# Turning one of the five long expert turns of a mixture-of-experts layer into a short one

## The chip, the cores and the metric

The kernel runs on one core of a Trainium2 chip, as one program. The metric is the device time of one execution in microseconds, as the median of several runs. Five engines matter here: TensorE (PE, with its weight loads PEld), VectorE (DVE), ScalarE (ACT), GpSimd (POOL) and SyncE (SP), whose queue issues nearly all transfers from HBM. "Weight load" is used below only for PE's own loads; what SP brings from HBM is called a load of expert weights.

## The reference, cut to what matters

A two-layer network on 256 tokens of width 1024 (and 256 context tokens in layer 0). Layer 1 ends with eight experts, of which each token takes two. Everything is in float32.

```python
def swiglu(h, w1, w3, w2):
    return (jax.nn.silu(h @ w1) * (h @ w3)) @ w2

def moe_swiglu(h, router_w, w1, w3, w2):
    t = h.reshape(B * L, D)                       # 256 x 1024
    logits = (t @ router_w).astype(jnp.float32)
    top_v, top_i = lax.top_k(logits, TOP_K)       # TOP_K = 2
    gates = jax.nn.softmax(top_v, axis=-1)
    ...
    for e in range(N_EXPERTS):                    # w1, w3: 1024 x 3584, w2: 3584 x 1024
        out = out + combine[:, e:e + 1] * swiglu(t, w1[e], w3[e], w2[e])
```

256 tokens with two experts each make 512 pairs, 64 an expert on average.

## The kernel before, in words

The program first computes layer 0 and the mixer of layer 1, and then the eight experts in eight **turns**, 0 to 7, one expert a turn. Before the first turn has gone far, a plan made on the chip (`plan`) counts the tokens of each expert and hands the experts to the turns. Expert 0 always has turn 0, since its weights are on the way before the router is done; the others are ranked by their number of tokens, and `RANKS` says which rank goes to which turn.

A turn has room for 128 or 64 tokens, by the table `TURNS`. The code of the two kinds differs:

- In a **long** turn (128) float32 products are made of three products of split numbers. The raw weights of a load are copied by ACT to a rounded high part (`hi`) and subtracted by DVE to a low part (`lo`); PE multiplies the tokens' high part by `hi` and by `lo` (lines 1590 and 1591) and the tokens' low part by `hi` (line 1594). The down products are the three lines of `mm3` (156 to 158). Raw room is free for the next load when DVE has made `lo`.
- In a **short** turn (64) there is no split: PE multiplies the raw float32 weights, with the 64 tokens in one half of the array's columns for one half of a load and in the other half for the other (lines 1582 and 1614). Raw room is free when PE has multiplied.

An expert's weights come in four chunks of its 3584 hidden columns (1024, 1024, 1024, 512). The turn goes over the chunks: the up products of chunk c with `w1` and `w3`, then the down products of the chunk before it with `w2`; the down products of a turn's last chunk come after the next turn's first up products. Each load is 1 MB, 42 loads a turn whatever its kind. `gather` collects the next turn's tokens during chunk 2, `finish` spreads a turn's rows back to the tokens (`macc`) during the first chunks of the next turn.

SP issues the loads strictly in the order of use. Their room is a ring of 12 tiles of 1 MB (`rr` and `raw`; 14 at first and 11 late in the last turn), so that a load is issued when the load 12 places ahead of it has let go of its room. In a long turn the high parts are made for up to two loads beyond the one that PE works on (`AHI`), the low parts for one (`ALO`).

```python
NRM, NHM, NLM, AHI, ALO = 12, 3, 2, 2, 1
            while len(his) + len(ahead) < AHI:
            while his and len(ahead) < ALO:
```

After the eight turns the program looks at two numbers of the plan: by how many tokens the fullest turn exceeds its room, and whether an expert has more than 128. If the first is above 0, a **second pass** computes all eight experts anew, with room for 128 in every turn (`tc.If(over > room)`).

Of the kernel before, what the change touches and what calls it, by code (L numbers as in the profile page):

```python
# [31 lines left out]
NHB = 4  # L32


TURNS = (128, 64, 128, 128, 64, 128, 128, 64)
LONG, SHORT = iter((0, 1, 2, 3, 4)), iter((5, 6, 7))
RANKS = [next(LONG) if n == 128 else next(SHORT) for n in TURNS]

CHUNKS = [(0, 1024), (1024, 1024), (2048, 1024), (3072, 512)]
# [3 lines left out]
def host_consts():  # L43
# [16 lines left out]
    i8 = np.arange(8)  # L60
    rt = np.concatenate([(i8[None, :] < i8[:, None]).reshape(-1), np.arange(1, 129), RANKS, TURNS, i8, 1024 * (i8 == 0)])
    return {
# [9 lines left out]
def hybrid_kernel(ctx: ExitStack, tc: tile.TileContext, a: dict, out: bass.AP, dbg=None, upto="end"):  # L72
# [1677 lines left out]
    def by_number(t, e):  # L1750
        return pm[:, t, e:e + 1]

    expert_pass(0, TURNS, number, by_turn,
                lambda t, e: comb[:, t, 0:1] if e == 0 else turns[:, 2 + t, e:e + 1])
# [39 lines left out]
```

## Time and profile before

| what | value |
|---|---|
| median of 3 runs | 1711.8 us (1709.98 to 1712.49) |
| the profiled execution | 1708.4 us |
| its span (first to last instruction) | 1706.6 us |
| granted TensorE clock, mean over the span | 0.992 of full speed |
| PE busy | 1653.8 us (97%) |
| DVE busy | 1152.3 us (68%) |
| ACT busy | 810.9 us (48%) |
| HBM read | 476.37 MB, 280 GB/s over the span |

Busy PE is not PE at its peak, because the records of overlapping matmuls are laid end to end, and the shares are means over a long front part (to about 796 us) and the eight expert turns after it. The table therefore says little about the turns; for these the rows below go stretch by stretch.

### The profile page before, as it was taken

The page shows a single profiled execution, that of the slowest core. Times are in us where ns is not written, and L with a number is a line of the kernel's source. Part 1 is how long each engine was busy: PE and PEld are TensorE (multiplying, and loading weights), DVE is VectorE, ACT ScalarE, POOL GpSimd, SP SyncE. Part 2 cuts the span into 40 slices and gives each one's busy share as a digit, 9 for nine tenths or more (in the row PEclk, how much of TensorE's full clock was granted, in tenths as well). Part 3 has the DMA queues.
Part 4 walks back from the last instruction along what each step waited for, and adds up shares of the span by engine and source line. Part 5 has one row for each costly group of instructions (what it writes and reads, how often), then busy time and mean ns, then how long its engine had stood idle before and what let it go on. Part 6 is the DMA issues. An engine that isn't in the chain of part 4 may idle for free.

```text
span 1706.6 us, 22066 instructions
## 1 busy us (share of the span) xinstructions
PE 1653.8 (97%) x8284; PEld 1238.7 (73%) x8284; DVE 1152.3 (68%) x1372; ACT 810.9 (48%) x941; POOL 26.8 (2%) x51
## 2 busy tenths in 40 slices
PE   7989999999999999999999999999999999999995
PEld 3767888788888888877786367888853578888532
DVE  3698897788566666856984148889841488898322
ACT  4633455322221357455773046777730467777201
POOL 1000000000000000000000000000000000000000
PEclk9999999999999999999999999999999999999997
DMA  9433375555565445337999999999999999999995
GB/s 367 150 101 123 99 253 162 167 187 174 184 198 185 152 145 179 113 132 283 327 357 337 409 410 412 408 411 376 342 354 408 412 411 409 411 375 347 355 406 197
DMA packets 186797, 479.03 MB, mean 281 GB/s; under 512 B 11761, under 2 KB 65201, under 8 KB 172081
## 3 DMA queue, kind: packets, MB, share of 16 engines
q1 hardware_dynamic: 185040, 473.80, 75.7%
q10 hardware_dynamic: 1074, 2.72, 0.5%
q8 instruction: 69, 1.13, 0.3%
q0 software_dynamic: 560, 0.94, 0.2%
q14 instruction: 54, 0.44, 0.1%
HBM read 476.37 MB, written 1.05 MB: 280 GB/s over the span
## 4 chain that ended last, share of the span: by engine, by line
PE 87%; DVE 5%; DMA 4%; ACT 2%; issue 1%; SPq 1%; POOL 0%; DVEq 0%; ACTq 0%; POOLq 0%
PE mm L156 9%; PE mm L157 8%; PE mm L158 8%; PE h L1582 8%; PE h L1591 7%; PE h L1594 7%; PE h L1590 7%; PE y L156 6%; PE y L157 6%; PE y L158 6%; PE y L1614 2%; DMA raw<-moe_w 2%; PE sc L589 1%; DMA rr<-moe_w 1%; PE sc L1561 1%
## 5 line engine op out<-in xcount | busy, mean ns | idle before, releaser
L145 ACT ACTIVATE hi<-raw 128x1024 fp32r<-128x1024 f32 x127 | 134.5, 1060 | 310.2 <-PE mm L157 99.0
L177 DVE TENSOR_TENSOR rb<-raw,rb 128x2048 fp32r<-128x2048 f32 x86 | 196.5, 2289 | 57.3 <-ACT rb L177 39.2
L1591 PE MATMUL h<-rb,hg 128*128 128x512 f32 x560 | 218.8, 391 | 2.6 <-DVE rb L177 2.5
L149 DVE TENSOR_TENSOR lo<-raw,hi 128x1024 fp32r<-128x1024 f32 x127 | 155.3, 1224 | 88.6 <-ACT hi L145 85.4
L177 ACT ACTIVATE rb<-raw 128x2048 fp32r<-128x2048 f32 x86 | 165.0, 1918 | 63.5 <-PE h L1594 28.5
L422 DVE SCALAR_TENSOR_TENSOR rr<-rr,cs,rr 128x512 f32<-128x512 f32 x256 | 181.8, 747 | 10.1 <-DMA rr<-b_mod 4.6
L156 PE MATMUL mm<-hbk,hi 128*128 128x512 f32 (+1 forms) x456 | 166.5, 366 | 0.9 <-DVE tm L829 0.8
L157 PE MATMUL mm<-hbk,hi 128*128 128x512 f32 (+1 forms) x456 | 163.7, 359 | 0.5 <-DVE hbk L305 0.5
L158 PE MATMUL mm<-hbk,lo 128*128 128x512 f32 (+1 forms) x456 | 163.7, 359 | 0.0
L177 DVE TENSOR_TENSOR rb<-rr,rb 128x2048 fp32r<-128x2048 f32 x50 | 114.4, 2290 | 34.0 <-ACT rb L177 24.1
L1590 PE MATMUL h<-rb,hg 128*128 128x512 f32 x352 | 130.9, 393 | 0.0
L1591 PEld LDWEIGHTS h<-rb,hg 128*128 128x128 f32 x560 | 105.1, 188 | 27.9 <-DVE rb L177 4.6
L177 DVE TENSOR_TENSOR rb<-raw,part 128x2048 fp32r<-128x2048 f32 x51 | 116.7, 2288 | 10.0 <-ACT part L177 4.3
L177 DVE TENSOR_TENSOR sil<-sil,h 128x512 f32<-128x512 f32 (+1 forms) x47 | 31.4, 669 | 127.2 <-PE h L1582 112.5
L177 ACT ACTIVATE part<-raw 128x2048 fp32r<-128x2048 f32 x51 | 97.7, 1916 | 39.7 <-PE h L1594 16.6
L177 ACT ACTIVATE rb<-rr 128x2048 fp32r<-128x2048 f32 x50 | 95.9, 1918 | 37.5 <-PE h L1594 15.7
L157 PE MATMUL y<-rb,ht 128*128 128x512 f32 x280 | 109.7, 392 | 0.0
L1594 PE MATMUL h<-rb,hg 128*128 128x512 f32 x352 | 107.0, 390 | 2.5 <-DVE hg L177 2.5
L1582 PE MATMUL h<-raw,hgs 128*64 128x512 f32 (+1 forms) x512 | 103.9, 541 | 0.0
L156 PEld LDWEIGHTS mm<-hbk,hi 128*128 128x128 f32 x456 | 85.8, 189 | 16.2 <-issue 2.4
L157 PEld LDWEIGHTS mm<-hbk,hi 128*128 128x128 f32 x456 | 86.0, 189 | 14.2 <-issue 1.0
L158 PEld LDWEIGHTS mm<-hbk,lo 128*128 128x128 f32 x456 | 86.0, 189 | 13.0
(381 smaller groups left out, 3087.2 us busy)
## 6 DMA issues: line engine op xcount, KB each, us to landing
raw<-moe_w SPq DMA_DIRECT2D x212, 1024.0 KB
rr<-moe_w SPq DMA_DIRECT2D x110, 1024.0 KB
rr<-w_mod SPq DMA_DIRECT2D x80, 512.0 KB
raw<-ffn_w SPq DMA_DIRECT2D x72, 512.0 KB
raw<-w_in SPq DMA_DIRECT2D x32, 512.0 KB
raw<-w_out SPq DMA_DIRECT2D x23, 512.0 KB
raw<-moe_w SPq DMA_DIRECT2D x12, 512.0 KB
rb<-w_mod SPq DMA_DIRECT2D x5, 1024.0 KB
```

What stands on the lines that cost most here:

```text
L145: ins = nc.scalar.activation(hi, raw, AF.Copy).ins
L149: nc.vector.tensor_tensor(lo, raw, hi.bitcast(F32), op=OP.subtract)
L156: nc.tensor.matmul(ps, lh, rh, start=start, stop=False)
L157: nc.tensor.matmul(ps, lh, rl, start=False, stop=False)
L158: nc.tensor.matmul(ps, ll, rh, start=False, stop=stop)
L177: r = getattr(self.engine, name)(*args, **kw)
L422: nc.vector.scalar_tensor_tensor(accs[x], rv[:, k, :], cs[:, x * 8 + kb:x * 8 + kb + 1], accs[x], op0=OP.mult, op1=OP.add)
L1582: nc.tensor.matmul(H[i][0][x * 64:x * 64 + 64, :n], HG[e][:, k0 + j, :], hi[:, j, x * n:(x + 1) * n], start=(k0 + j == 0), stop=(k0 + j == 7))
L1590: nc.tensor.matmul(H[i][b], hgh[:, kb, :], hi[:, j, bc], start=(kb == 0), stop=False)
L1591: nc.tensor.matmul(H[i][b], hgh[:, kb, :], lo[:, j, bc], start=False, stop=False)
L1594: nc.tensor.matmul(H[i][b], hgl[:, kb, :], hi[:, j, bc], start=False, stop=(kb == 7))
L1614: nc.tensor.matmul(Y[e][0][hh * 64:hh * 64 + 64], ht[:, j0 + j, half], hi[:, j, xc], start=on, stop=off)
```

## The change

One of the long turns becomes short. Turn 3 goes from 128 to 64 places, and the order of kinds goes from long, short, long, long, short, long, long, short to a strict alternation. The ranking follows: the four fullest (expert 0 counted first) have the long turns, the four others the short ones.

```diff
-TURNS = (128, 64, 128, 128, 64, 128, 128, 64)
-LONG, SHORT = iter((0, 1, 2, 3, 4)), iter((5, 6, 7))
+TURNS = (128, 64, 128, 64, 128, 64, 128, 64)
+LONG, SHORT = iter((0, 1, 2, 3)), iter((4, 5, 6, 7))
 RANKS = [next(LONG) if n == 128 else next(SHORT) for n in TURNS]
```

The kinds of the turns, before and after: 0 L L, 1 S S, 2 L L, 3 L S, 4 S L, 5 L S, 6 L L, 7 S S. So turns 3 to 5 hold L S L before and S L S after.

On PE, the first up products of turn 3, just behind the last down products of turn 2's chunk 2 (`rb` is split weights, `ht` the hidden rows, `hg` a long turn's tokens). Before:

```order
L158 MATMUL y<-rb_8723,ht 128x512
L1590 MATMUL h<-rb_8746,hg 128x512
L1591 MATMUL h<-rb_8766,hg 128x512
L1590 MATMUL h<-rb_8746,hg 128x512
L1591 MATMUL h<-rb_8766,hg 128x512
L1594 MATMUL h<-rb_8746,hg 128x512 x2
```

The same place after, where `raw` and `rr` are the raw weights of the ring and `hgs` a short turn's tokens:

```order
L158 MATMUL y<-rb_8718,ht 128x512
L1582 MATMUL h<-raw,hgs 64x512 x5
L1582 MATMUL h<-rr_8762,hgs 64x512 x4
L1582 MATMUL h<-rr_8768,hgs 64x512 x4
L1582 MATMUL h<-raw,hgs 64x512 x8
L1582 MATMUL h<-rr_8789,hgs 64x512 x4
L1582 MATMUL h<-rr_8795,hgs 64x512 x4
```

One load that took 12 matmuls takes 4, and PE reads the ring itself. From the gather for turn 3 to the gather for turn 4, PE's list of instructions after is the one that before stands from the gather for turn 4 to that for turn 5, instruction for instruction; the next turn after is likewise the one before of turn 5.

On SP's queue, the loads that take over the room of turn 3's first five loads (what each waits for stands behind it: the DMA queue that it uses, and the engine that gives the room free). Before:

```order
L128 DMA raw<-moe_w 128x2x1024 [waits DMAHW6_49,DVE_49]
L128 DMA raw<-moe_w 128x2x1024 [waits DMAHW7_49,DVE_49]
L128 DMA rr_9031<-moe_w 128x2x1024 [waits DMAHW0_49,DVE_49]
L128 DMA rr_9058<-moe_w 128x2x1024 [waits DMAHW1_49,DVE_49]
L128 DMA raw<-moe_w 128x2x1024 [waits DMAHW2_49,DVE_49]
```

After:

```order
L128 DMA raw<-moe_w 128x2x1024 [waits DMAHW6_49,PE_49]
L128 DMA raw<-moe_w 128x2x1024 [waits DMAHW7_49,PE_49]
L128 DMA rr_8879<-moe_w 128x2x1024 [waits DMAHW0_49,PE_49]
L128 DMA rr_8894<-moe_w 128x2x1024 [waits DMAHW1_49,PE_49]
L128 DMA raw<-moe_w 128x2x1024 [waits DMAHW2_49,PE_49]
```

The loads, their sizes and their order stay; what they wait for moves from DVE's split to PE's products.

## Rows read from the trace of the kernel before

**Rows 1.** The page's 40 slices of the span (42.7 us each).

```profile
PEclk9999999999999999999999999999999999999997
DMA  9433375555565445337999999999999999999995
GB/s 367 150 101 123 99 253 162 167 187 174 184 198 185 152 145 179 113 132 283 327 357 337 409 410 412 408 411 376 342 354 408 412 411 409 411 375 347 355 406 197
```

**Rows 2.** Windows, one a turn, turns 1 to 7.

```profile
core 0: us, PE busy (x) PEld busy (x) DVE busy (x) ACT busy (x) POOL busy (x), PEclk, DMA share, GB/s
916.80:1004.90 88.10, 85.72 (x433) 35.82 (x433) 14.79 (x18) 16.18 (x24) 0.00 (x0) 1.00 1.00 395
1004.90:1129.60 124.70, 124.55 (x568) 98.81 (x567) 105.02 (x64) 89.03 (x66) 0.00 (x0) 1.00 1.02 410
1129.60:1253.90 124.30, 124.30 (x575) 102.46 (x574) 106.35 (x66) 87.00 (x64) 0.00 (x0) 1.00 0.97 367
1253.90:1342.40 88.50, 86.12 (x433) 36.58 (x431) 13.35 (x18) 15.33 (x23) 0.00 (x0) 1.00 0.99 393
1342.40:1468.50 126.10, 124.54 (x568) 98.80 (x567) 106.45 (x64) 89.89 (x66) 0.00 (x0) 1.00 1.02 411
1468.50:1592.80 124.30, 124.30 (x575) 102.46 (x575) 106.41 (x66) 86.99 (x64) 0.00 (x0) 1.00 0.98 369
1592.80:1706.60 113.80, 92.65 (x431) 36.22 (x429) 27.11 (x60) 14.68 (x24) 2.54 (x2) 0.91 0.81 316
```

**Rows 3.** DMA issues by line: number, size of each.

```profile
raw<-moe_w SPq DMA_DIRECT2D x212, 1024.0 KB
rr<-moe_w SPq DMA_DIRECT2D x110, 1024.0 KB
```

**Rows 4.** Windows from 881 us to the last loads, columns as in rows 2.

```profile
881.00:930.00 49.00, 49.00 (x242) 34.65 (x242) 29.26 (x20) 25.94 (x25) 0.00 (x0) 1.00 0.89 323
930.00:1150.00 220.00, 217.46 (x1028) 147.01 (x1025) 135.10 (x88) 116.55 (x96) 0.00 (x0) 1.00 1.02 410
1150.00:1215.00 65.00, 65.00 (x296) 53.92 (x295) 59.65 (x39) 47.85 (x33) 0.00 (x0) 1.00 1.00 380
1215.00:1265.00 50.00, 50.00 (x243) 35.90 (x243) 30.00 (x22) 26.92 (x25) 0.00 (x0) 1.00 0.88 312
1265.00:1490.00 225.00, 221.06 (x1045) 148.92 (x1042) 137.59 (x90) 118.22 (x97) 0.00 (x0) 1.00 1.02 410
1490.00:1555.00 65.00, 65.00 (x297) 53.92 (x296) 59.49 (x39) 47.57 (x33) 0.00 (x0) 1.00 1.00 380
1555.00:1605.00 50.00, 50.00 (x242) 35.34 (x242) 30.23 (x21) 27.30 (x25) 0.00 (x0) 1.00 0.90 317
1605.00:1682.00 77.00, 74.61 (x364) 30.03 (x360) 16.60 (x30) 6.15 (x11) 0.00 (x0) 1.00 1.02 406
```

**Rows 5.** SP queue's waits: 1165 to 1215 us (a long turn), then 960 to 975 (short).

```profile
SPq L128 <- DVE rb L177: 39.8, 18, 4.0
...
SPq L128 <- PE h L1582: 10.7, 4, 6.3
```

**Rows 6.** Windows of 5 us about the stall's start, columns as in rows 2.

```profile
1150.00:1155.00 5.00, 5.00 (x25) 4.24 (x24) 4.77 (x5) 3.39 (x3) 0.00 (x0) 1.00 1.02 421
1155.00:1160.00 5.00, 5.00 (x25) 4.15 (x25) 4.66 (x3) 3.80 (x4) 0.00 (x0) 1.00 1.01 415
1160.00:1165.00 5.00, 5.00 (x25) 4.09 (x24) 4.17 (x5) 3.90 (x4) 0.00 (x0) 1.00 1.00 390
```

**Rows 7.** Timeline where turns 2 and 5 begin: start, us, instruction, idle before it.

```profile
1003.44 2.29 DVE L177 TENSOR_TENSOR rb<-rr,rb 128x2048 fp32r<-128x2048 f32 x1 [6.04 <-ACT rb L177]
1005.78 0.50 PE L1591 MATMUL h<-rb,hg 128*128 128x512 f32 x1 [0.15 <-DVE rb L177]
...
1344.72 0.50 PE L1591 MATMUL h<-rb,hg 128*128 128x512 f32 x1 [1.56 <-DVE rb L177]
```

**Rows 8.** The chain that ended last: two pieces of its end.

```profile
1672.77 9.29 DMA raw<-moe_w
...
1682.10 1.10 PE y L1614 x4
```

## The prediction, on record before the changed kernel ran

> **What bounds the kernel now.** I read the 40 slices first [rows 1]. TensorE's granted clock is full in all but the last, so no stage differs by clock. The transfers show two kinds of slices in the back half: ten at 408 to 412 GB/s, and two groups of three at 342 to 376. Something is full in the first kind and held back in the second.
>
> Next the windows by turn [rows 2]. A long turn takes PE 124.3 us (turns 3 and 6, in which PE has no idle time by these rows), a short one 88.1 (turn 1) or 88.5 (turn 4). A turn's weights are 42 loads of 1.0486 MB [rows 3], 44.04 MB; at 410 GB/s that is 107.4 us. So a long turn is bound by PE (124.3 against 107.4) and gains 16.9 us of loads on PE; a short turn is bound by the transfers (107.4 against 88.1) and uses 19.3 us of such a stock up. Before, the pattern long, long, short has 336.7 us of PE work (2 x 124.3 + 88.1) against 322.2 of transfers: bound by PE, with transfers that must stop for 14.5 us a round. The stock that a second long turn in a row would lay by does not fit into the ring.
>
> That stop is in the windows of rows 4: 410 GB/s for 220 us and again for 225, then 380 for 65 us and 312 or 317 for 50 us, each time. In the slow stretches SP waits for DVE's splits, that is for room [rows 5], 39.8 us of 50; so the transfers are held back, they don't hold back PE. At the end the transfers lead again: the last load is on the chain, issued at 1672.77 and landed 9.29 us later, and PE's last down products start on it at 1682.10 [rows 8].
>
> **The change part by part.** Turn 3 becomes short. It *removes* the work of a long turn and *adds* that of a short one; 42 splits on ACT and on DVE fall away, which counts nothing in time, since neither is waited for in turns 3 and 6 (DVE is busy 102.46 of 124.3 us, ACT 87.00 [rows 2]). The other turns keep their work and change their places. The loads keep number, size and order. Nothing changes before turn 3's gather, in turn 2.
>
> *PE's side.* One long turn less and one short turn more: 124.3 - 88.1 = 36.2 us.
>
> *The transfers' side.* A round of long and short is now 212.4 us of PE against 214.8 us of transfers, so from turn 1 on the transfers should run at 410 GB/s without a stop, and the end follows them. From 930 to 1605 us the rows 4 show 220 x 410 + 65 x 380 + 50 x 312 + 225 x 410 + 65 x 380 + 50 x 317 = 263,300 (us x GB/s, so 263.3 MB) in 675 us. At 410 GB/s throughout they take 642.2 us: 32.8 us less. The rest, from 1605 on, is the last short turn with transfers at 406 already, and behind it the tail; both are the same afterwards.
>
> The smaller saving decides, as both chains must end: 32.8 us.
>
> *What the moved border costs.* The trace has no border from long to short that begins with room in the ring. The three that it has begin with a full one and lose 10.4 us of transfers (881 to 930, 49 us at 323), 12.0 (1215 to 1265) and 11.3 (1555 to 1605) [rows 4]. There is a reason for a loss: in a short turn a room is free only when PE has multiplied, in a long one when DVE has split [rows 5], a load or so ahead of PE. The first split of turn 2 ends at 1005.73 (1003.44 + 2.29) just ahead of the matmul that uses it [rows 7]; once loads lie ready, `ALO` lets it run one load ahead, 124.3 / 42 = 3.0 us. So rooms come back some 3 to 4 us later at the border. Is there slack for that? Turn 2 starts at 1004.9 with its first split just in time [rows 7], so without a stock. Full speed lasts until 1160 (421 and 415, then 390 [rows 6]): 155 us, in which 63.6 MB come and PE uses 155.1 / 124.5 x 44.04 = 54.9, so the ring holds a stock of 8.7 MB, 21.2 us. At 1129.6, where turn 3 now begins to draw it down, the stock is 124.7 - 107.4 = 17.3 us. Slack 3.9 us against a delay of 3 to 4: the transfers just about get by. The bounds are nothing and 11.2 us (mean of the three) for each of the three borders behind 930 us (turns 3, 5 and 7). I take 0.5 us each, near the lower end, since the stock is that far below the full ring: 1.5 us.
>
> *The border from short to long.* Twice before, at turns 2 and 5, PE waits for the first split, 0.15 and 1.56 us [rows 7]. After it happens at turns 2, 4 and 6. Where the transfers lead, this wait is part of their time and not on top of it: 0, at most 1.56 more.
>
> *The sum.* 32.8 - 1.5 = 31.3 us. Against the profiled execution: 1708.4 - 31.3 = 1677.1 us (1.8 us of it lie outside the span of 1706.6). That execution is 3.4 us below the median of the runs shown, 1711.8, within which I state the forecast: **1680.5 us**, 1.8% faster.
>
> The bandwidth is the figure that carries the sum, and there a rule of the Trainium skill speaks against the change. "DMA: Bandwidth & Descriptors", section "Where 436 GB/s comes from", says that "for HBM↔SBUF transfers the HBM side (~358) binds". By that rule a turn's weights would take an estimated 123 us whatever its kind, and a short turn would buy nothing. The trace disagrees, with 410 GB/s over 220 and 225 us [rows 4]; the skill's "HBM Reference", section "Specifications (TRN2)", agrees with the trace in that it gives a core that streams alone about 425.
>
> **The rivals.**
>
> *The border from long to short costs its full price wherever it stands.* Then the loss belongs to the change of kind and not to the full ring. For it: two thirds of the loss in rows 4 (23.3 of 32.8 us) lies at the borders at turns 4 and 7. Against it: the rule by which rooms come free explains 4 us of delay and not 11. Three borders at 11.2 us cost 33.6 where 32.8 are saved: 1712 to 1713 us, no change.
>
> *Transfers can't hold 410 GB/s.* If the slow stretches are a limit that comes with long streaming, the 263.3 MB take 263,300 / 352 = 748 us (352 is the mean of the slow stretches, 65 us at 380 and 50 at 312 or 317), 73 more than the 675 before: 1785 us, **slower**. The rule of the Trainium skill's DMA page, above, would show in this way. Against it: the rate returns to 410 as soon as PE draws faster, at 1265, and the transfer engines have idle time in the slow stretches (share 0.88 and 0.90 against 1.02 [rows 4]). It decides as soon as a window behind 1130 us shows less than 390 with SP not waiting for room.
>
> *The second pass runs.* `RANKS` now needs the fifth expert in the order to have at most 64 tokens; with 65 the program computes all eight experts once more in long turns. Price: 8 x 124.3 = 994 us, about 2675 us, **slower** by half. This is no matter of the trace: evaluating the reference's router on its inputs gives 60, 55, 43, 85, 89, 53, 59 and 68 tokens for experts 0 to 7. Behind expert 0 they rank 89, 85, 68, 59, 55, 53, 43, so the fifth has 59. The smallest gap between a token's second and third logit is 0.006, so six more tokens don't move by rounding.
>
> *PE stays the bound.* If the transfers turned out quicker than 410 (two windows of 5 us show 415 and 421 [rows 6]), PE's saving would be all: 36.2 us, 1675.6. This is the lower end.
>
> **How the numbers follow.** The forecast, with borders that cost little, has 0.88 (it covers 1675 to 1692: PE's saving at one end, one border at its full 11.2 us at the other). The border's full price everywhere has 0.05, the transfers' limit 0.03, the second pass 0.02; a partial case, two borders at full price (1702), 0.02. A change of less than 0.2% (3.4 us) can't be told from none here. So the range is 1674 to 1692, and faster has 0.92 (0.88, 0.02 and a share of the border's case), same 0.03, slower 0.05.
>
> **What would show it.** Windows from 930 us to the last load at 405 to 411 GB/s, without the four stretches at 312 to 380. Turn starts (first products of each) at about 1130, 1219, 1344, 1434 and 1559: rounds of 215 us. Last down products at about 1650 and a span of 1675. SP's waits for DVE's splits much shorter, with those for PE's short products in their place. At the starts of turns 4 and 6 PE waits for a split by one or two us. Wrong would be the step on the border if the 40 us about turns 3, 5 and 7 show less than 390 GB/s; the step on the transfers if they run at 410 and PE has idle time of more than some 3 us a round all the same; the plan if there is work behind 1700 us.

## The result, and the profile after

| what | before | after |
|---|---|---|
| median | 1712.1 us (1709.98 to 1712.79, 4 runs) | 1678.8 us (1676.46 to 1679.86, 4 runs) |
| ratio of the runs, as recorded | | 0.9816 (95%: 0.9805 to 0.9828) |
| the profiled execution, its span | 1708.4 us, 1706.6 us | 1679.9 us, 1678.1 us |
| PE busy | 1653.8 us | 1620.3 us |
| DVE, ACT busy | 1152.3, 810.9 us | 1049.4, 726.0 us |

The kernel became 1.84% faster by the recorded ratio and 1.95% by the two medians; 1.8% was forecast (1680.5 us, range 1674 to 1692). The 40 slices of the page after (42 us each) answer to [rows 1]:

```profile
PEclk9999999999999999999999999999999999999998
DMA  9524375556666534545898999999999999999995
GB/s 362 164 85 131 113 250 167 153 180 184 189 198 191 155 126 137 177 164 196 323 359 314 400 408 413 407 411 407 408 411 411 409 390 408 410 414 406 387 405 199
```

The two groups of three slices at 342 to 376 GB/s are gone. From the 23rd slice to the last but one two are below 400, with 390 and 387. The windows after say it by turn and then by stretch. The columns are those of [rows 2]: first the seven turns from turn 1 on, then the whole stretch in which the transfers should hold 410, then the 20 or 40 us about the starts of turns 3, 5 and 7, the stretch to the last loads, and last pieces of 5 us at the starts of turns 4 and 6.

```profile
916.30:1004.40 88.10, 85.72 (x434) 35.83 (x433) 15.20 (x18) 16.59 (x24) 0.00 (x0) 1.00 1.00 391
1004.40:1129.50 125.10, 125.10 (x569) 98.06 (x568) 101.50 (x63) 83.21 (x62) 0.00 (x0) 1.00 1.02 410
1129.50:1218.30 88.80, 86.17 (x434) 36.58 (x432) 13.37 (x18) 15.33 (x23) 0.00 (x0) 1.00 1.02 407
1218.30:1346.80 128.50, 126.91 (x567) 99.19 (x568) 103.31 (x63) 84.54 (x62) 0.00 (x0) 0.99 1.02 410
1346.80:1436.70 89.90, 86.19 (x434) 36.60 (x432) 13.37 (x18) 15.33 (x23) 0.00 (x0) 1.00 1.01 400
1436.70:1565.20 128.50, 126.91 (x566) 99.21 (x567) 103.29 (x63) 84.55 (x62) 0.00 (x0) 0.99 1.02 410
1565.20:1678.10 112.90, 92.12 (x431) 35.81 (x429) 27.17 (x60) 14.68 (x24) 2.55 (x2) 0.94 0.82 321
...
930.00:1590.00 660.00, 648.09 (x3044) 412.50 (x3044) 353.96 (x244) 300.74 (x257) 0.00 (x0) 0.99 1.02 407
...
1130.00:1150.00 20.00, 20.00 (x91) 9.65 (x89) 5.18 (x3) 5.22 (x5) 0.00 (x0) 1.00 1.02 400
...
1330.00:1370.00 40.00, 40.00 (x178) 23.59 (x178) 16.65 (x11) 13.46 (x11) 0.00 (x0) 1.00 1.00 390
...
1550.00:1590.00 40.00, 40.00 (x179) 22.82 (x179) 16.48 (x11) 11.88 (x10) 0.00 (x0) 1.00 0.98 384
1590.00:1655.00 65.00, 62.33 (x310) 22.91 (x306) 12.38 (x25) 4.96 (x9) 0.00 (x0) 1.00 1.00 397
...
1220.00:1225.00 5.00, 4.40 (x12) 3.52 (x13) 3.50 (x3) 2.94 (x3) 0.00 (x0) 0.66 1.02 409
1435.00:1440.00 5.00, 2.08 (x6) 1.13 (x5) 3.10 (x2) 3.71 (x3) 0.00 (x0) 0.90 1.03 410
1440.00:1445.00 5.00, 5.00 (x18) 4.04 (x17) 3.73 (x2) 3.56 (x2) 0.00 (x0) 0.76 1.03 410
```

The reader sees two things. The transfers run at 407 GB/s over 660 us, where the same stretch of loads before was an average of 390 (263.3 MB in 675 us). And what is missing to 410 lies at the borders from long to short: 400, 390 and 384, not the 312 to 323 of [rows 4]. Short turns take 88.1 to 89.9 us; the long turns 4 and 6 take 128.5, where [rows 2] has 124.3 to 126.1.

SP's waits over the whole span, by what they wait for (us in total, times, longest), say what holds the loads back now. After:

```profile
SPq L128 <- DVE rb L177: 275.9, 114, 12.2
...
SPq L128 <- PE h L1582: 146.9, 86, 8.0
```

and the same two rows of before:

```profile
SPq L128 <- DVE rb L177: 400.8, 171, 12.2
...
SPq L128 <- PE h L1582: 118.9, 69, 7.8
```

The wait for splits fell by 125 us, that for the short products rose by 28. The chain that ended last shows who leads (start, length, piece): at the starts of turns 4 and 6 it passes from a load over ACT's and DVE's split to PE, and at the end it goes over the last load, as in [rows 8].

```profile
1197.50 18.79 DMA rr<-moe_w
1216.31 1.92 ACT rb L177
1218.25 2.30 DVE rb L177
...
1414.71 19.97 DMA rr<-moe_w
1434.71 1.92 ACT rb L177
1436.65 2.30 DVE rb L177
...
1645.13 10.12 DMA raw<-moe_w
1655.30 1.10 PE y L1614 x4
```

### The profile page after: what moved, and what is told of

The parts are those of the page before. It is cut to its first block, busy times and chain, and to the rows that moved or that the text cites. A ratio compares the mean times of both kernels' runs of the same rounds, so it can differ in the third digit from the quotient of the medians.

```text
span 1678.1 us, 21544 instructions
## 1 busy us (share of the span) xinstructions
PE 1620.3 (97%) x8134; PEld 1168.2 (70%) x8134; DVE 1049.4 (63%) x1318; ACT 726.0 (43%) x890; POOL 26.9 (2%) x51
## 4 chain that ended last, share of the span: by engine, by line
PE 87%; DVE 5%; DMA 3%; ACT 2%; issue 1%; SPq 0%; POOL 0%; DVEq 0%; ACTq 0%; POOLq 0%
PE h L1582 11%; PE mm L156 9%; PE mm L157 9%; PE mm L158 8%; PE h L1591 6%; PE h L1594 6%; PE h L1590 6%; PE y L156 5%; PE y L157 5%; PE y L158 5%; PE y L1614 4%; DMA rr<-moe_w 2%; PE sc L589 1%; PE sc L1561 1%; PE sc L1383 1%
## 5 line engine op out<-in xcount | busy, mean ns | idle before, releaser
L177 DVE TENSOR_TENSOR rb<-raw,rb 128x2048 fp32r<-128x2048 f32 x73 | 167.1, 2290 | 79.8 <-ACT rb L177 59.6
L1591 PE MATMUL h<-rb,hg 128*128 128x512 f32 x448 | 177.2, 395 | 4.1 <-DVE rb L177 4.0
L177 ACT ACTIVATE rb<-raw 128x2048 fp32r<-128x2048 f32 x73 | 139.9, 1917 | 50.7 <-PE h L1594 31.9
L1582 PE MATMUL h<-raw,hgs 128*64 128x512 f32 (+1 forms) x720 | 143.4, 529 | 0.0
L1590 PE MATMUL h<-rb,hg 128*128 128x512 f32 x288 | 109.1, 399 | 1.6 <-ACT rb L177 1.6
L1582 PEld LDWEIGHTS h<-raw,hgs 128*64 128x64 f32 x720 | 51.6, 137 | 77.5 <-issue 68.9
L1591 PEld LDWEIGHTS h<-rb,hg 128*128 128x128 f32 x448 | 85.2, 190 | 26.1 <-DVE rb L177 6.3
L177 DVE TENSOR_TENSOR rb<-raw,part 128x2048 fp32r<-128x2048 f32 x42 | 96.1, 2288 | 10.5 <-PE h L1591 4.6
L177 DVE TENSOR_TENSOR rb<-rr,rb 128x2048 fp32r<-128x2048 f32 x35 | 80.0, 2288 | 27.2 <-ACT rb L177 23.7
L177 ACT ACTIVATE part<-raw 128x2048 fp32r<-128x2048 f32 x42 | 80.4, 1914 | 36.4 <-DMA raw<-moe_w 17.0
L1594 PE MATMUL h<-rb,hg 128*128 128x512 f32 x288 | 88.5, 393 | 2.5 <-DVE hg L177 2.5
L157 PE MATMUL y<-rb,ht 128*128 128x512 f32 x224 | 87.6, 391 | 0.0
```

What stands on the lines that cost most here:

```text
L157: nc.tensor.matmul(ps, lh, rl, start=False, stop=False)
L177: r = getattr(self.engine, name)(*args, **kw)
L1582: nc.tensor.matmul(H[i][0][x * 64:x * 64 + 64, :n], HG[e][:, k0 + j, :], hi[:, j, x * n:(x + 1) * n], start=(k0 + j == 0), stop=(k0 + j == 7))
L1590: nc.tensor.matmul(H[i][b], hgh[:, kb, :], hi[:, j, bc], start=(kb == 0), stop=False)
L1591: nc.tensor.matmul(H[i][b], hgh[:, kb, :], lo[:, j, bc], start=False, stop=False)
L1594: nc.tensor.matmul(H[i][b], hgl[:, kb, :], hi[:, j, bc], start=False, stop=(kb == 7))
```

## The experiments

The theory: after turn 1 there are two chains, PE's work and the transfers, both must end, the ring's stock couples them, and after the change the transfers lead. The rivals of the prediction are a price of the border that doesn't depend on the ring, a limit of the transfers, the second pass, and PE as the bound. Diffs are against the changed kernel. Kernels were timed beside the kernel before, and ratios are to that, as recorded; the quotient of two medians can differ from them by 0.001. "..." in a diff marks lines left out.

**The order alone.** The alternation up to turn 6, but five long turns, so that turns 6 and 7 are both long.

```diff
-TURNS = (128, 64, 128, 64, 128, 64, 128, 64)
-LONG, SHORT = iter((0, 1, 2, 3)), iter((4, 5, 6, 7))
+TURNS = (128, 64, 128, 64, 128, 64, 128, 128)
+LONG, SHORT = iter((0, 1, 2, 3, 4)), iter((5, 6, 7))
```

> Five long and three short turns as before the change, in the order long, short, long, short, long, short, long, long: the alternation without the fourth short turn. Theory (PE's sum and the transfers' sum are two chains, and the greater decides): PE's work is that of before, five long and three short turns, so the end is PE's, whatever the transfers save: turns 0 to 6 start as after the change (turn 7 at about 1565 us), then a long turn of 124 us and a tail, 1705 to 1718 us, ratio 0.996 to 1.004. Rival (the alternation is what pays, since it keeps the ring from filling): about 1680 us, ratio 0.98.

Measured: 1718.7 us, ratio 1.0055 (1.0038 to 1.0072), slightly above the range that was expected. The windows of its last two turns and of a stretch near its end (columns as above):

```profile
1437.70:1564.00 126.30, 124.66 (x567) 98.84 (x568) 106.48 (x65) 89.86 (x66) 0.00 (x0) 1.00 1.02 410
1564.00:1692.00 128.00, 127.52 (x568) 103.72 (x567) 117.20 (x90) 91.27 (x70) 0.00 (x0) 1.00 0.80 284
1610.00:1680.00 70.00, 69.52 (x308) 55.73 (x307) 65.09 (x58) 48.74 (x39) 0.00 (x0) 1.00 0.79 260
```

Turn 7 begins at 1564.0, as early as after the change (1565.2), and is then a long turn on which PE works without a pause while the transfers drop to 260 GB/s. There PE leads. In turns 1 to 6 the transfers lead: these turns take 646.2 us (turn 1 begins at 917.8) for 637.2 us of PE's work (3 x 88.1 + 3 x 124.3), where before the change they took 676.0 for 673.4. So with the old work this order makes PE wait 9.0 us in turns 1 to 6 instead of 2.6, and the last long turn doesn't make that up. It is therefore not the greater of two sums over the whole kernel that decides, but the chain that leads in each stretch; after the change that is the transfers from turn 1 on.

**The number alone.** Four long turns, but two long ones and two short ones in a row.

```diff
-TURNS = (128, 64, 128, 64, 128, 64, 128, 64)
+TURNS = (128, 64, 128, 128, 64, 64, 128, 64)
```

> Four long and four short turns as after the change, in the order long, short, long, long, short, short, long, short: turns 3 and 4 change places. PE's work is the same as after. Theory (a stock of loads beyond the ring's room stops the transfers, and what they lose there is missing when they lead again): the two long turns in a row lose about 16 us of transfers (4.8 in the second half of turn 3 and 11.6 at the border to turn 4, as before the change), against 3 to 5 us at the borders of the alternation; the two short turns in a row then run dry. About 1690 us (1685 to 1697), ratio 0.987. Rival (PE's sum decides, so the number of short turns is all): 1677 to 1681 us, ratio 0.9815.

Measured: 1694.6 us, ratio 0.9912 (0.9896 to 0.9929). Its windows of turns 3 to 6:

```profile
1132.00:1256.30 124.30, 124.30 (x576) 102.47 (x575) 106.29 (x66) 87.00 (x64) 0.00 (x0) 1.00 0.97 364
1256.30:1344.10 87.80, 85.42 (x433) 36.70 (x433) 12.31 (x17) 11.63 (x20) 0.00 (x0) 1.00 1.00 396
1344.10:1452.30 108.20, 89.58 (x427) 30.32 (x423) 7.79 (x14) 11.13 (x20) 0.00 (x0) 1.00 1.02 410
1452.30:1581.50 129.20, 127.67 (x566) 99.71 (x567) 103.28 (x63) 84.55 (x62) 0.00 (x0) 0.97 1.02 411
```

This is the theory in four rows. The second long turn in a row can't lay by what it gains: 364 GB/s, which loses (410 - 364) / 410 x 124.3 = 13.9 us of transfers. The second short turn in a row finds no stock and takes 108.2 us at 410 GB/s; 107.4 was worked out for a turn that the transfers lead. The kernel is 15.8 us behind the changed one, near those 13.9. So order alone is worth +0.55%, number alone -0.9%, both -1.8%: the two effects don't add up to the gain.

**Less work for PE.** In turns 4 and 6 the third up product (line 1594) is left out, so that the output lacks that term; PE then has some 25 us less to do in each.

```diff
+                lean = base == 0 and e in (4, 6)
...
-                    for j in range(nk):
+                    for j in range(0 if lean else nk):
```

> The changed kernel, with the third up product (the tokens' low part by the weights' high part) left out in the long turns 4 and 6: 112 matmuls at 0.227 us, some 25 us of PE work less in each, so that those turns need less of PE (about 99 us) than of the transfers (107). Theory (the transfers lead from turn 1 on): the end moves only by what the stock's overflow and the clock cost, 1672 to 1677 us, ratio 0.977 to 0.980. Rival (PE leads, and the transfers just keep up): 50 us less, about 1629 us, ratio 0.952.

Measured: 1677.2 us, ratio 0.9814 (0.9798 to 0.9831), the changed kernel's time. Some 50 us less of PE's work (by the number of products; PE's busy time in the two turns fell by 19 and 18 us) leave the ratio where it was (0.9814 against 0.9816), so the transfers lead; the rival "PE the bound" falls. Turn 4 takes 116.8 us for 128.5, turn 5 behind it 98.2 for 89.9, together 215.0, where the forecast has rounds of 215. The window from 930 to 1590 us:

```profile
930.00:1590.00 660.00, 627.40 (x2882) 368.91 (x2878) 353.87 (x248) 300.30 (x259) 0.00 (x0) 1.00 1.02 410
```

**A ring of ten places** instead of 12.

```diff
-NRM, NHM, NLM, AHI, ALO = 12, 3, 2, 2, 1
+NRM, NHM, NLM, AHI, ALO = 10, 3, 2, 2, 1
```

> The changed kernel with two places of 1 MB less in the ring of raw weights (10 instead of 12). Theory (the border from long to short costs only what the long turn's stock exceeds the ring's room): 5.1 us of room less at each of the borders to turns 1, 3, 5 and 7, so each loses 4 to 5 us more: 1692 to 1700 us, ratio 0.988 to 0.993. Rival (the border's cost belongs to the change of kind, whatever the room): within 3 us of the changed kernel, 1676 to 1682 us, ratio 0.9815. Rival (PE leads): the same.

Measured: 1706.0 us (10 runs), ratio 0.9978 (0.9968 to 0.9987): 27 us slower than the changed kernel, more than expected, and nearly all that the change had gained. Its windows of turns 1 and 3, of the whole stretch, and about the start of turn 5:

```profile
917.80:1011.50 93.70, 86.90 (x434) 35.37 (x433) 13.34 (x18) 15.31 (x23) 0.00 (x0) 1.00 1.00 397
1140.00:1234.30 94.30, 87.43 (x433) 36.04 (x431) 13.32 (x17) 15.32 (x23) 0.00 (x0) 1.00 0.99 394
...
930.00:1590.00 660.00, 634.41 (x2956) 403.29 (x2954) 347.67 (x239) 295.42 (x252) 0.00 (x0) 0.99 1.00 396
...
1320.00:1385.00 65.00, 65.00 (x307) 45.28 (x305) 37.54 (x26) 31.68 (x29) 0.00 (x0) 1.00 0.96 363
```

Two places less are 2 x 2.56 = 5.1 us of stock (1.0486 MB at 410 GB/s each), and a short turn is longer by about as much: 5.6, 5.5, 4.5 and 5.0 us for turns 1, 3, 5 and 7, together 20.6 of the 26.4 between the two spans; the long turns have 4.3, the front part 1.5. The short turns' share is just above what was expected (four times 4 to 5); the rest I had not counted. About the start of turn 5 the loads now run at 363 GB/s: what the ring can't hold is lost there.

**The changed kernel once more**, timed together with the next two.

> The changed kernel itself, as the measure for the two runs beside it: 1676 to 1681 us, ratio 0.980 to 0.983. At the starts of turns 4 and 6 the granted clock falls for one record of 3.4 us, as in its first profile, or falls at one of them only.

Measured: 1678.8 us, ratio 0.981 (0.9796 to 0.9823). Its profile differs a little from the first: the whole stretch, the three borders, and the start of turn 6.

```profile
930.00:1590.00 660.00, 649.11 (x3062) 411.47 (x3060) 355.28 (x245) 301.24 (x258) 0.00 (x0) 1.00 1.02 409
1130.00:1150.00 20.00, 20.00 (x86) 8.62 (x86) 4.72 (x3) 4.19 (x3) 0.00 (x0) 1.00 1.00 395
1330.00:1370.00 40.00, 40.00 (x178) 24.65 (x178) 17.96 (x11) 14.63 (x12) 0.00 (x0) 1.00 1.02 406
1550.00:1590.00 40.00, 40.00 (x179) 22.38 (x180) 16.00 (x11) 11.43 (x9) 0.00 (x0) 1.00 1.02 408
...
1435.00:1440.00 5.00, 3.13 (x15) 0.96 (x12) 2.29 (x1) 3.81 (x2) 0.00 (x0) 1.00 1.02 407
1440.00:1445.00 5.00, 5.00 (x23) 4.12 (x24) 4.58 (x2) 3.63 (x3) 0.00 (x0) 1.00 1.02 409
```

Here the borders lose 1.6 us in all ((410 - 409) / 410 x 660), against 4.8 us at 407 in the first profile; as the rows give whole GB/s, either figure is good to 0.8 us. The fall of the clock that was expected at turn 4 or 6 is not in this profile.

**Work for PE in its wait.** Eight products that nothing reads, in PE's queue ahead of the first product of turns 4 and 6, where PE waited in the first profile after.

```diff
+                if base == 0 and e in (4, 6) and (c, i, k0) == (0, 0, 0):
+                    w = scps()
+                    for _ in range(WARM):
+                        nc.tensor.matmul(w, hi[:, 0, 0:128], hi[:, 0, 0:512], start=True, stop=True)
```

> The changed kernel with eight matmuls more, of no use for the output, at the starts of turns 4 and 6, which PE can do once the first split's high part is there and before its low part is (1.8 us each time, in an idle time of 1.6 us). Theory (transfers lead, and PE's halt at these starts matters only as more stock at the next border): the clock stays at full speed, the long turns 4 and 6 shrink by 1 to 2 us, and the end moves by 0 to 3 us, 1674 to 1680 us. Rival (the fall of the clock is what makes these turns 128.5 us long instead of 124.3, and PE leads): 4 us and more less, under 1675 us.

Measured: 1678.9 us, ratio 0.9808 (0.9794 to 0.9821), no change. The eight products (line 1590 of this run's kernel) run where PE had waited, 1.6 us at a time, and the first product of the turn follows them at 1224.76. The rows are those products at turn 4, then turns 4, 5 and 6, each long turn counted from its first extra product:

```profile
1222.80 2.11 PE L1590 MATMUL sc<-rb 128*128 128x512 f32 x8 [0.17 <-ACT rb L178]
...
1222.80:1350.00 127.20, 127.20 (x575) 99.66 (x576) 103.34 (x63) 84.57 (x62) 0.00 (x0) 1.00 1.02 410
1350.00:1438.70 88.70, 86.13 (x433) 36.55 (x431) 13.34 (x18) 15.32 (x23) 0.00 (x0) 1.00 1.02 406
1438.70:1565.90 127.20, 127.20 (x575) 99.65 (x576) 103.36 (x63) 84.60 (x62) 0.00 (x0) 1.00 1.02 410
```

The turns are as long as in the second profile of the changed kernel (127.0, 88.8, 126.9), only that PE is busy all through the long ones: the work fits into the wait and costs nothing. The expected shrinking of the long turns by 1 to 2 us shows only against the first profile (128.5), whose clock fell there. The rival of this run, PE leading with a kernel under 1675 us, falls.

**A ring of 13 places, second pass left out.** One place more, for which room is taken from the second pass and from an early load's place.

```diff
-NRM, NHM, NLM, AHI, ALO = 12, 3, 2, 2, 1
+NRM, NHM, NLM, AHI, ALO = 13, 3, 2, 2, 1
...
-    heads = [(lambda t=t: mb.tile([128, 2048], F32, name="head", tag=t), n) for t, n in (("macc", MA), ("hg1", 0))]
+    heads = [(lambda t=t: mb.tile([128, 2048], F32, name="head", tag=t), n) for t, n in (("macc", MA),)]
...
-def hybrid_kernel(ctx: ExitStack, tc: tile.TileContext, a: dict, out: bass.AP, dbg=None, upto="end"):
+def hybrid_kernel(ctx: ExitStack, tc: tile.TileContext, a: dict, out: bass.AP, dbg=None, upto="nofb"):
```

> The changed kernel with one place more in the ring (13 instead of 12). To make room it leaves out the second pass, which these inputs don't reach. Theory (what is left of the loss at the borders is stock beyond the ring's room): 2.6 us of room more at each border, so the stretches about turns 3, 5 and 7 stand nearer to 410 GB/s and the transfers end 2 to 4 us earlier: 1673 to 1678 us, some 3 us under the changed kernel beside it. Rival (the borders cost what they cost by the change of kind): the same as the changed kernel within 1 us.

Measured: 1666.6 us, ratio 0.9736 (0.9723 to 0.975), 12 us under the changed kernel and below the range that was expected, more than a border's remainder can give. So one of its two edits had an effect of its own.

**The second pass left out alone**, with 12 places (the last edit of the diff above only). The 8 and 14 us named below are some 9 and 17 by the two traces.

> The changed kernel with its ring of 12, and without the second pass, which these inputs don't reach: the control for the run with 13 places, which left the second pass out too. If the 12 us that the run with 13 places gained are the ring's: 1676 to 1680 us, as the changed kernel. If the end of the program is shorter without the two branches behind the last output (between the last product and the end of the span stood 8 us in that run, 14 in the changed kernel): 1671 to 1674 us, and the ring's share is 5 to 8 us.

Measured: 1670.1 us, ratio 0.9765 (0.9752 to 0.9778). So the pass that never runs costs 8.7 us (1678.8 - 1670.1; 7.7 by the ratios), and the 13th place is worth 1670.1 - 1666.6 = 3.5 (5.0 by the ratios). I had not foreseen the first when I ran the 13 places. The timeline places it: the last work that either profile shows is the issue of the last output, here ACT's of the changed kernel (span 1678.1 us)

```profile
1666.15 0.39 ACTq L1735 DMA_DIRECT2D out<-res  x1
```

and here of the kernel without the pass (span 1668.3 us):

```profile
1664.00 0.39 ACTq L1735 DMA_DIRECT2D out<-res  x1
```

Behind it there are 1678.1 - 1666.5 = 11.6 us with the pass and 1668.3 - 1664.4 = 3.9 without: 7.7 of the 8.7 us stand there, where the changed kernel loads the two numbers and jumps over the pass twice. Which of these steps costs how much the profile doesn't show. The kernel before has the same code and 12.2 us behind its last output, so that the comparison of before and after is not touched.

**13 places with the second pass kept.** The tokens of the odd long turns, which only the second pass has, borrow a ring place.

```diff
+        if e % 2:
+            if not spare:
+                spare.append(places["raw"].pop(0)[0])
+            hg = spare[0]().bitcast(F32R).rearrange("p (x k t) -> p x k t", x=2, k=KB)
...
```

> The changed kernel with 13 places in the ring and with the second pass kept. The room comes from the token tile of the odd turns, which under the alternation holds 64 tokens only; the second pass, in which odd turns are long, takes a place of the ring for it instead. Theory (one place more is worth some 1.5 to 2.6 us at each of the borders to turns 1, 3, 5 and 7): 1670 to 1674 us, ratio 0.976 to 0.979, faster than the changed kernel by 5 to 8 us. Rival (what the run with 13 places gained came from leaving out the second pass): 1677 to 1680 us.

Measured: 1675.2 us, ratio 0.9795 (0.9781 to 0.9808). It computes all that the changed kernel does and is the quickest that does; its interval overlaps that of the changed kernel (0.9805 to 0.9828, and 0.9796 to 0.9823), so that a gain of some 3 us is likely and not certain. It lies between what the theory (1670 to 1674) and the rival (1677 to 1680) had. The window shows where the gain would come from:

```profile
930.00:1590.00 660.00, 651.34 (x3070) 412.74 (x3070) 356.72 (x248) 302.00 (x259) 0.00 (x0) 1.00 1.02 410
```

About turns 5 and 7 nothing is lost (411 GB/s over 65 us each), about turn 3 a little (405 over 55 us). Counted from the start of turn 1 to the last output, which leaves out the front part and the second pass, the profiles of the two runs with 13 places have 742.8 and 742.3 us, and four with 12 places have 745.9 (the second profile of the changed kernel), 746.4 (with work in PE's wait), 746.8 (without the second pass) and 750.3 (the first profile). There the place is worth 3 us and more, by one execution in each profile.

**A turn too few.** Three long and five short turns, so that the expert with 68 tokens doesn't fit into its turn and the second pass runs; then the same with 13 places.

```diff
+TURNS = (128, 64, 128, 64, 64, 64, 128, 64)
+LONG, SHORT = iter((0, 1, 2)), iter((3, 4, 5, 6, 7))
```

> Five short turns, in the order long, short, long, short, short, short, long, short: the fourth expert in the order, with 68 tokens, now gets a turn of 64 places. By the plan's rule the second pass runs: the eight experts anew in long turns, 8 x 124.3 = 994 us and some 30 to 60 us to fill the ring again: 2680 to 2740 us. Without the second pass (if the rule weren't as read): about 1675 us.

> The kernel with 13 places and five short turns, so that the second pass runs with its borrowed place: 994 us and 30 to 60 us to fill the ring on top, 2670 to 2700 us, a few us under the same order of turns with 12 places (2689.5).

Measured: 2689.5 us and 2683.1 us, one execution each, both as expected. The first is 1010.7 us above the changed kernel; 994 was worked out for the second pass. The first pass ends where that of the changed kernel does (the last products, line 1453, begin at 1657.9 against 1657.2), though a fifth turn is short: where the transfers lead, 36.2 us less of PE's work buy nothing. In the second pass's 900 us from 1700 on PE has no pause:

```profile
1700.00:2600.00 900.00, 900.00 (x4182) 752.14 (x4181) 797.63 (x489) 673.37 (x495) 0.00 (x0) 1.00 0.98 364
```

## Why the prediction was right

**Two chains, the smaller saving decides: right.** The transfers lead from turn 1 to the end. Taking 25 us of PE's work out of each of two turns changes nothing, nor does a fifth short turn, and a turn without a stock takes 108.2 us.

**The transfers' 32.8 us: right in size.** The stretch runs at 407 and 409 GB/s in two profiles. From the start of turn 1 to the end of the span it was 1706.6 - 916.8 = 789.8 us before; after, it is 1678.1 - 916.3 = 761.8 in the first profile and, with turn 1 starting at 919.4, 1677.0 - 919.4 = 757.6 in the second. That is 28.0 and 32.2 us less, with 31.3 forecast. What the prediction took as the same afterwards nearly is: the last 65 us of loads run at 396 GB/s in the first profile and ran at 403 before, 1.1 us more, and behind the last load stand 22.8 us for 24.5. The rival of a limit that comes with long streaming falls: 407 GB/s over 660 us bring some 269 MB, and where the rate is lower, SP waits for room (11.3 of the 14 us from 1563 on, 12.4 of the 14 from 1346 on, for the short turn's products). The rule of the Trainium skill ("DMA: Bandwidth & Descriptors", "Where 436 GB/s comes from") by which the HBM side binds at about 358 does not hold in this kernel, by these rates.

**The border from long to short: 1.5 us forecast for three, 4.8 and 1.6 measured.** This term was too small in the first profile and right in the second. By the sign that the prediction set (less than 390 GB/s in the 40 us about a short turn's start) the step was wrong at turn 7 of the first profile, with 384; turn 5 had 390, and in the second profile these stretches have 406 and 408. The mechanism, a stock that nearly fills the ring, holds by both sides of it: two places less bring windows of 363 GB/s and 27 us, one more brings 410 over the whole stretch and some 3.5 us. So the rival of a full price at every border (11.2 us) falls. What was mis-sized is the stock: the slack of 3.9 us was worked out for a long turn of 124.7 us, at whose end the stock is 17.3. Turns 4 and 6 took 127 us in the second profile (stock 127.0 - 107.4 = 19.6) and 128.5 in the first (21.1, with room for 21.2), and the borders behind them lost 0.4 and 0.2 us there and 2.0 and 2.5 here. A plain function of the turn's length it is not: behind turn 2, with 125.5 and 125.1 us, 0.7 and 0.5 us were lost. How late a room comes back at the border was not measured by itself.

**The border from short to long: nothing forecast, and nothing seen by itself.** PE waits there, as the prediction said it would, at turns 4 and 6 (start, length, instruction, idle before it):

```profile
1218.28 0.73 PE L1590 MATMUL h<-rb,hg 128*128 128x512 f32 x2 [0.24 <-ACT rb L177]
1220.60 0.79 PE L1591 MATMUL h<-rb,hg 128*128 128x512 f32 x1 [1.59 <-DVE rb L177]
...
1436.67 0.73 PE L1590 MATMUL h<-rb,hg 128*128 128x512 f32 x2 [1.32 <-ACT rb L177]
1439.00 0.80 PE L1591 MATMUL h<-rb,hg 128*128 128x512 f32 x1 [1.59 <-DVE rb L177]
```

At turn 2, where the prediction had a wait too, there is next to none (PE is busy for all of 125.1 us in the first profile and for 125.4 of 125.5 in the second). The wait is part of the transfers' time: filling it with work changes nothing. It is however what makes the long turn longer, and so the stock, which the term above did not count.

**The turn starts.** The starts of turns 3, 5 and 7 are put 2.9 us behind their first product, among the last down products of the turn before, as [rows 2] has it for turns 4 and 7. Forecast 1130, 1219, 1344, 1434 and 1559; measured 1129.5, 1218.3, 1346.8, 1436.7 and 1565.2. The first two fit; from turn 5 on they are 3 to 6 us late. Here the forecast counted long turns of 125 us; in the second profile they took 127.0 and 126.9. The last down products start at 1655.3 for 1650, the span is 1678.1 for 1675. PE is idle for 4.2 and 5.3 us in the rounds of turns 3 and 4 and of 5 and 6, and 4.2 in both in the second profile, more than the 3 us that the prediction gave as a sign against the step on the transfers. The sign was set too low: the 88.1 us that it took for a short turn's work hold 2.4 us of idle time already (PE busy 85.72), and 2.4 more are what a round of 214.8 leaves.

**The sum.** The profiled execution gained 28.5 us and 31.3 was forecast; between the medians it is 33.4. The forecast of 1680.5 lies 1.7 above the median. Of this closeness a part is luck: the two profiled executions stand 3.7 us under and 1.1 over their medians.

**Second pass: as counted.** There is no work of it in the trace after, and its price, 994 us, is near the 1010.7 of the run in which it happens.

## What to carry to other kernels

Where stages with two different bounds take turns, add up each chain over a whole round and let stages of either kind alternate singly: what one stage lays by for the next can't exceed the buffer, and the buffer's room in microseconds (here 12 loads of 2.56 us, less what is in flight and in use) is to be set against the stage's surplus. A removed stage is then worth the smaller of the two savings, and only if the order lets the stock through; where the lead passes from one chain to the other on the way, the waits of both add up, so number and order have to be tried together. A fallback that never runs is worth timing too: here it costs 8.7 us, 7.7 of them behind the last store.

## What the runs showed of the hardware that was not expected

The granted clock fell at the start of turns 4 and 6 of the first profile after, and nowhere else in turns 1 to 6. The window of 5 us from 1220 has 0.66, the two from 1435 have 0.90 and 0.76: (0.10 + 0.24) x 5 x 2 = 3.4 us at the lower of the two levels, 1.2 GHz for 2.4, and 0.34 x 5 x 2 = 3.4 at turn 4. Ahead of the fall in turn 6 PE had waited 1.32 and 1.59 us with 0.73 us of work between them, ahead of that in turn 4 0.24 and 1.59. In the second profile of the same kernel the waits at turn 6 were 0.27 and 1.59 us, and the windows have 1.00: the same program has the fall in one execution and not in another, behind waits as long as at turn 4.

Each fall takes 3.4 us at half speed, so 1.7 us of PE's time, from a long turn: 128.5 us with it, 127.0 and 126.9 without. The transfers at the borders behind these turns had 390 and 384 GB/s with it, 406 and 408 without. Whether the one causes the other is not shown; it would fit, since a PE that is later gives its rooms back later. From the start of turn 1 on the first profile is 4.2 us longer than the second (761.8 against 757.6), but the second reached turn 1 3.1 us later, so that the spans differ by 1.1. In the medians nothing stands out: with work in PE's wait, where the rows of the profiled execution show the clock at 1.00 over turns 4 and 6, it is 1678.9 us, and without it 1678.8. In how many of the other executions the clock fell there is not recorded.
